# A hybrid streaming-encoder layer on one core: the order of the first loads, two products on zeros, and x scaled on two engines

## The chip, the cores and the metric

The kernel runs on one core of one Trainium2 chip. The metric is the device time of one execution in microseconds; the median of the runs is what counts, and lower is better.

## The reference, cut to what matters

One layer is computed for 512 tokens of width 2048, in float32. The opening, which the change touches, computes the RMS-normalised input `h` and the per-layer embedding `e`:

```
h = rmsnorm(x, g_pre)                 # x: 512 x 2048
proj = h @ w_in                       # feeds a gated DeltaNet branch and a conv branch
... mixers, gates, w_br_a, w_br_b, w_out ...
x = x + rmsnorm(mixed, g_post)
e = p @ w_ple_proj                    # p: 512 x 256, w_ple_proj: 256 x 2048
x = x + rmsnorm(sigmoid(x @ w_ple_gate) * e, g_ple)
```

`e` depends on nothing but `p` and one weight, so the kernel computes it at the very start, while `x` is still arriving, and parks it in DRAM until the end.

## The kernel before, in words

Every large product is a float32 product made from three products of a reduced type: each operand is split into a high part (`hi`, a cast on ACT) and a low part (`lo`, a subtraction on DVE or POOL), and TensorE (PE) multiplies high by high, high by low and low by high into the same bank. Weights stream through `prep()` (lines 115 to 131): a DMA of 512 KB into one of three `raw` tiles, then two pieces, each with a cast into `hi` (L127) and a subtraction into `lo` (L128), into a ring of four `w` tiles. All the DMAs named here are issued from one queue, SP's.

The opening is `load_x()` (lines 226 to 266). Its parts:

- `embed_in()` loads the two halves of the transposed p (`pr`, 256 KB each, L201) and splits them into `ph` (ACT, L203) and `pl` (DVE, L205).
- `embed(j, ...)` for the four column blocks j of `w_ple_proj`: 24 products of 128x512 each (L216, L217, L218), three for each of two depths k and four token tiles, into four banks; then four copies out of the banks, on ACT and DVE in turn (L221). The opening's pool of banks, `xps`, has six.
- For each of the four token tiles of x: two DMAs of 512 KB (L237), two squares with a running sum on ACT (L245), the mean and epsilon on DVE (L247, L248), the power -1/2 on POOL (L250), and two scalings in place on DVE (L252).
- Then 64 transposes on PE (L261), four for each of 16 column tiles, with a scaled copy `hh` on ACT (L264) and its remainder `hl` on DVE (L265). They need the identity matrix (`cst[:, 0:128]`) and the gains in `vec`.
- The 16 blocks of e are written to DRAM by SP (L257), and the rest of the constants is loaded.

After that come `gemm_cm` jobs (products `g`, lines 184 to 188) on w_in, first for the gate of the conv branch, then `z_phase` and everything else. The jobs pull weight pieces from the same ring.

The program order is not the final order. A scheduler goes over the program with a model of its own, starts on each engine whatever comes first in program order among what is ready in that model, and so fixes the order of each engine's queue before the run. The SP queue of before, for instance, holds the second half of p behind the first two DMAs of x, though the program has it ahead of them. On the chip each queue runs in its fixed order.

Of the kernel before, what the change touches and what calls it, by code (L numbers as in the profile page):

```python
# [9 lines left out]
F32 = mybir.dt.float32  # L10
F32R = mybir.dt.float32r
AF = mybir.ActivationFunctionType
ALU = mybir.AluOpType
AX = mybir.AxisListType.X

P = 128
T = 512
NTT = T // P
# [20 lines left out]
V_DW = V_CONV + QKV_TILES * 4  # L39
# [42 lines left out]
def _body(ctx, tc, A, out):  # L82
    nc = tc.nc
    PSUM = bass.MemoryType.PSUM
    mm = nc.tensor.matmul

    const = ctx.enter_context(tc.tile_pool(name="const", bufs=1, side="right"))
    rawp = ctx.enter_context(tc.tile_pool(name="rawp", bufs=3, side="right"))
    ring = ctx.enter_context(tc.tile_pool(name="ring", bufs=4))
    hpool = ctx.enter_context(tc.tile_pool(name="hpool", bufs=32))  # L90
    slots = ctx.enter_context(tc.tile_pool(name="slots", bufs=21, side="right"))
# [2 lines left out]

    cst = const.tile([P, C_COLS], F32, name="cst")
    vec = const.tile([P, V_COLS], F32, name="vec")
    nc.sync.dma_start(cst[:, 0:P], A["consts"][:, 0:P])
    ident = cst[:, C_ID:C_ID + P]
    half_c = const.tile([P, 8], F32, name="half_c")
    nc.gpsimd.memset(half_c, 0.5)  # L100
# [8 lines left out]
    def vv(col, n=1):  # L109
        return vec[:, col:col + n]  # L110


    prep_src = deque()
    prepped = deque()
    low_part = [nc.vector]

    def prep():
        if not prep_src:
            return
        src = prep_src.popleft()  # L120
        raw = rawp.tile([P, 1024], F32, tag="raw", name="raw", bufs=3)
        nc.sync.dma_start(raw, src)
        for q in range(2):
            rq = raw[:, q * T:(q + 1) * T]
            w = ring.tile([P, 1024], F32R, tag="w", name="w")
            hi, lo = w[:, 0:T], w[:, T:]
            nc.scalar.copy(hi, rq)  # L127
            low_part[0].tensor_tensor(lo, rq, hi.bitcast(F32), ALU.subtract)  # L128
            hi_lo[id(hi)] = w.rearrange("p (s c) -> p s c", s=2)
            prepped.append((hi, lo))  # L130
# [64 lines left out]
    pe_dram = dram.tile([4, NTT, P, T], F32, name="pe_dram")  # L195

    def embed_in():
        pT = []
        for k in range(2):
            pr = slots.tile([P, T], F32, tag="s", name="pr")  # L200
            nc.sync.dma_start(pr, A["pT"][k])  # L201
            ph = slots.tile([P, T], F32R, tag="s", name="ph")
            nc.scalar.copy(ph, pr)  # L203
            pl = slots.tile([P, T], F32R, tag="s", name="pl")
            nc.vector.tensor_tensor(pl, pr, ph.bitcast(F32), ALU.subtract)  # L205
            pT.append((ph, pl))
        return pT

    def embed(j, pT, xps):
        ps = [xps.tile([P, T], F32, tag="xp", name="e_ps") for _ in range(NTT)]  # L210
        for k in range(2):
            wh, wl = prepped.popleft()
            lh, ll = pT[k]
            for tt in range(NTT):
                b = slice(tt * P, (tt + 1) * P)
                mm(ps[tt], lh[:, b], wh, start=k == 0, stop=False)  # L216
                mm(ps[tt], lh[:, b], wl, start=False, stop=False)  # L217
                mm(ps[tt], ll[:, b], wh, start=False, stop=k == 1)  # L218
        for tt in range(NTT):
            e = slots.tile([P, T], F32, tag="s", name="e_sb")  # L220
            (nc.vector.tensor_copy if tt % 2 else nc.scalar.copy)(e, ps[tt])  # L221
            e_sb[j, tt] = e
# [3 lines left out]
    def load_x():  # L226
        with tc.tile_pool(name="xin", bufs=1) as xin, tc.tile_pool(name="xps", bufs=6, space=PSUM) as xps:
            xs = []
            H = D // 2
            prep_src.extend(A["w_ple_proj"][j] for j in range(4))  # L230
            prep_src.extend(first_src)
            pT = embed_in()
            prep()
            for tt in range(NTT):
                xt = xin.tile([P, D], F32, name=f"x{tt}")
                for hf in range(2):
                    nc.sync.dma_start(xt[:, hf * H:(hf + 1) * H], A["x"][tt * P:(tt + 1) * P, hf * H:(hf + 1) * H])  # L237
                if tt == 2:
                    nc.sync.dma_start(vec[:, 0:V_DW], A["vecs"][:, 0:V_DW])
                prep()  # L240
                embed(tt, pT, xps)
                ss = small.tile([P, 2], F32, tag="xss", name="xss")
                junk = xin.tile([P, H], F32, name="xjunk")
                for hf in range(2):
                    nc.scalar.activation(junk, xt[:, hf * H:(hf + 1) * H], AF.Square, accum_out=ss[:, hf:hf + 1])  # L245
                ms = small.tile([P, 1], F32, tag="xms", name="xms")
                nc.vector.tensor_tensor(ms, ss[:, 0:1], ss[:, 1:2], ALU.add)  # L247
                nc.vector.tensor_scalar(ms, ms, 1.0 / D, EPS, ALU.mult, ALU.add)  # L248
                rs = small.tile([P, 1], F32, tag="xrs", name="xrs")
                nc.gpsimd.tensor_tensor(rs, ms, mhalf_c[:, 0:1], ALU.pow)  # L250
                for hf in range(2):
                    nc.vector.tensor_scalar(xt[:, hf * H:(hf + 1) * H], xt[:, hf * H:(hf + 1) * H], rs, None, ALU.mult)  # L252
                xs.append(xt)
            nc.sync.dma_start(cst[:, P:], A["consts"][:, P:])
            nc.sync.dma_start(vec[:, V_DW:], A["vecs"][:, V_DW:])
            for (j, tt), e in e_sb.items():
                nc.sync.dma_start(pe_dram[j, tt], e)  # L257
            for k in range(NK):
                ps = xps.tile([P, T], F32, tag="xp", name="xp")
                for tt in range(NTT):  # L260
                    nc.tensor.transpose(ps[:, tt * P:(tt + 1) * P], xs[tt][:, k * P:(k + 1) * P], ident)  # L261
                hh = hpool.tile([P, T], F32R, tag="h", name="hh")
                hl = hpool.tile([P, T], F32R, tag="h", name="hl")
                nc.scalar.activation(hh, ps, AF.Copy, scale=vv(V_GPRE + k))  # L264
                nc.vector.scalar_tensor_tensor(hl, ps, vv(V_GPRE + k), hh.bitcast(F32), ALU.mult, ALU.subtract)  # L265
                hT.append((hh, hl))
# [11 lines left out]

    first_src = [w_in_tile(ZB_TILE0)[0], w_in_tile(ZB_TILE0)[1]]
    load_x()  # L280


# [1055 lines left out]
    def load(jp, pr, q):  # L1338
        n = loads[0]
        loads[0] += 1  # L1340
        if n < 3 or n % 8 in (1, 4, 7):
            raw = rawp.tile([P, 1024], F32, tag="raw", name="raw", bufs=3)
        else:
            raw = s3.tile([P, 1024], F32, tag="rw", name="rw", bufs=5)
        src, blk = WHICH[pr]
        nc.sync.dma_start(raw, src[jp, blk, q])
        sources.append(raw)
# [272 lines left out]
    for tt in range(NTT):  # L1620
# [9 lines left out]
        for j in range(4):  # L1630
            s = e_t4[tt][j]
# [67 lines left out]
```

## Time and profile before

| | us |
|---|---|
| median of three runs | 2446.0 (2445.83 to 2446.65) |
| the profiled execution's own time | 2447.55 |
| its span, first to last instruction | 2445.8 |
| PE busy | 2414.0 (99% of the span) |
| DVE, ACT, POOL busy | 1792.4, 1208.8, 507.0 |
| first product of PE starts | 6.68 |
| embedding products end, transposes start | 32.04 |

The profiled execution took 1.55 us more than the median. Times inside a run are counted from the span's start. In a row of the timeline the first column is the start, the second how long the row lasted; a matmul's length holds the time to drain it, so the pace of PE is read from the distance between starts. "x2" at a row's end says that it stands for two instructions. In brackets stands how long the engine was idle before, and what it waited for.

### The profile page before, as it was taken

The numbers are of one execution on the slowest core, as the hardware profiler recorded it, in microseconds if no ns is written. First come the engines' busy times: TensorE is split into PE (matmuls) and PEld (weight loads), VectorE is DVE, ScalarE is ACT, GpSimd is POOL, SyncE is SP. The second block draws the span as 40 slices with busy tenths as digits, with TensorE's granted clock in tenths as the row PEclk, the third lists the DMA queues.
The fourth block names the chain that finished last, engine by engine and source line by source line (L and its number), as shares of the span: only waits on it lengthen the run. The fifth ranks groups of instructions, "written<-read, shape, count | busy, mean of one in ns | idle before, by whom it ended". The sixth has DMA issues, their size and how long they took to land.

```text
span 2445.8 us, 33732 instructions
## 1 busy us (share of the span) xinstructions
PE 2414.0 (99%) x11962; PEld 1985.5 (81%) x11962; DVE 1792.4 (73%) x3345; ACT 1208.8 (49%) x2357; POOL 507.0 (21%) x531
## 2 busy tenths in 40 slices
PE   8999999999999999999999998999999999999998
PEld 7888888887888888888888887888887888787886
DVE  7877888777677676867777678998998654667644
ACT  6455544554655656455555544454324533554532
POOL 0001110013213021132300005998740000000000
PEclk9999999999999999999999999999999999999999
DMA  7577776666536263556622222443534333665552
GB/s 270 162 199 199 202 201 208 207 162 204 175 119 185 87 185 93 171 168 178 181 90 90 67 91 79 138 137 104 170 118 166 131 122 99 232 216 173 188 173 77
DMA packets 145289, 380.21 MB, mean 155 GB/s; under 512 B 16352, under 2 KB 24800, under 8 KB 145120
## 3 DMA queue, kind: packets, MB, share of 16 engines
q1 hardware_dynamic: 119008, 319.32, 39.4%
q0 software_dynamic: 23808, 54.54, 10.3%
q10 hardware_dynamic: 2304, 4.20, 0.5%
q8 instruction: 94, 1.54, 0.3%
q14 instruction: 75, 0.61, 0.1%
HBM read 329.75 MB, written 48.23 MB: 155 GB/s over the span
## 4 chain that ended last, share of the span: by engine, by line
PE 89%; DVE 3%; POOL 2%; DMA 2%; issue 2%; ACT 2%; SPq 0%; POOLq 0%; DVEq 0%; ACTq 0%
PE g L186 13%; PE g L188 13%; PE g L184 13%; PE zp L423 6%; PE zp L421 6%; PE zp L422 5%; PE yp L1090 4%; PE yp L1094 4%; PE yp L1092 4%; PE f L1382 2%; PE f L1383 2%; PE f L1384 2%; PE f L1548 2%; PE f L1549 2%; PE f L1550 2%
## 5 line engine op out<-in xcount | busy, mean ns | idle before, releaser
L188 PE MATMUL g<-hh,w 128*128 128x512 f32 x1536 | 610.6, 397 | 4.1 <-POOL w L128 4.1
L186 PE MATMUL g<-hl,w 128*128 128x512 f32 x1536 | 611.3, 398 | 0.0
L184 PE MATMUL g<-hh,w 128*128 128x512 f32 x1536 | 609.5, 397 | 0.0
L127 ACT CAST w<-raw 128x512 fp32r<-128x512 f32 x588 | 357.9, 618 | 446.8 <-PE g L188 172.8
L128 DVE TENSOR_TENSOR w<-raw,w 128x512 fp32r<-128x512 f32 x464 | 321.5, 700 | 169.2 <-ACT w L127 166.6
L188 PEld LDWEIGHTS g<-hh,w 128*128 128x128 f32 x1536 | 289.8, 189 | 61.5 <-POOL w L128 5.4
L186 PEld LDWEIGHTS g<-hl,w 128*128 128x128 f32 x1536 | 289.6, 189 | 55.8 <-issue 1.4
L184 PEld LDWEIGHTS g<-hh,w 128*128 128x128 f32 x1536 | 289.9, 189 | 54.7 <-ACT w L127 0.9
L954 DVE SCALAR_TENSOR_TENSOR uc<-up,vec,uc 128x506 f32<-128x506 f32 (+29 forms) x390 | 284.0, 734 | 11.9
L128 POOL TENSOR_TENSOR w<-raw,w 128x512 fp32r<-128x512 f32 x124 | 161.4, 1314 | 136.7 <-DVE uc L954 74.5
L656 DVE SCALAR_TENSOR_TENSOR cv<-g,vec,cv 128x511 f32<-128x511 f32 x144 | 106.4, 739 | 27.2 <-ACT cv L654 26.6
L1090 PE MATMUL yp<-w,uh 128*128 128x512 f32 x256 | 100.2, 392 | 0.7 <-DVE gt L1102 0.7
L1094 PE MATMUL yp<-w,ul 128*128 128x512 f32 x256 | 100.1, 392 | 0.0
L1090 PE MATMUL yp<-w,oh 128*128 128x512 f32 x256 | 100.0, 393 | 0.0
L1092 PE MATMUL yp<-w,uh 128*128 128x512 f32 x256 | 100.0, 391 | 0.0
L1092 PE MATMUL yp<-w,oh 128*128 128x512 f32 x256 | 99.6, 389 | 0.0
L1094 PE MATMUL yp<-w,ol 128*128 128x512 f32 x256 | 99.1, 389 | 0.0
L842 DVE TENSOR_TENSOR prod<-UT,VT 128x2 f32<-128x2 f32 (+30 forms) x248 | 88.4, 356 | 6.5
L1006 POOL DMA_DIRECT2D wsum<-in_w_out x96 | 76.1, 847 | 71.2 <-DMA wsum<-in_w_out 32.9
L1326 POOL TENSOR_TENSOR rmsm<-totm,mhalf_c 128x2 f32<-128x2 f32 x2 | 2.4, 1198 | 378.3 <-DVE totm L1324 378.3
L973 POOL TENSOR_TENSOR uc<-uc,pr 128x511 f32<-128x511 f32 (+29 forms) x60 | 77.8, 1297 | 3.7 <-ACT pr L972 2.5
L1382 PE MATMUL f<-wsp,oph 128*128 128x512 f32 x192 | 75.6, 394 | 1.7 <-ACT wsp L1363 1.7
(386 smaller groups left out, 4952.5 us busy)
## 6 DMA issues: line engine op xcount, KB each, us to landing
raw<-in_w_in SPq DMA_DIRECT2D x194, 512.0 KB, 3.4
wsum<-in_w_out POOLq DMA_DIRECT2D x96, 256.0 KB, 5.4
raw<-in_w_ple_gate SPq DMA_DIRECT2D x40, 512.0 KB, 3.5
wo_sums<-wsum POOLq DMA_DIRECT2D x64, 256.0 KB, 4.1
raw<-in_w_br_a SPq DMA_DIRECT2D x32, 512.0 KB, 3.4
raw<-in_w_br_b SPq DMA_DIRECT2D x32, 512.0 KB, 3.3
raw<-in_w_ga SPq DMA_DIRECT2D x24, 512.0 KB, 4.7
raw<-in_w_gb SPq DMA_DIRECT2D x24, 512.0 KB, 4.5
```

The lines of the kernel that those rows point to most:

```text
L127: nc.scalar.copy(hi, rq)
L128: low_part[0].tensor_tensor(lo, rq, hi.bitcast(F32), ALU.subtract)
L184: mm(ps, wh, rh, start=(k == 0), stop=False)
L186: mm(ps, wh, rl, start=False, stop=False)
L188: mm(ps, wl, rh, start=False, stop=(k == NK - 1))
L421: mm(ps[pr][t], lh, wh, start=q + n == 0, stop=False)
L423: mm(ps[pr][t], lh, wl, start=False, stop=q == 3 and n == 1)
L954: pin(nc.vector.scalar_tensor_tensor(y[:, s:], u[:, 0:T - s], vv(w0 + TAPS - 1 - s), y[:, s:], ALU.mult, ALU.add))
L1090: mm(ps[tt], lh[:, b], wh, start=k == 0, stop=False)
L1092: mm(ps[tt], lh[:, b], wl, start=False, stop=False)
L1094: mm(ps[tt], ll[:, b], wh, start=False, stop=k == NK - 1)
L1382: mm(ps, lh, wh[:, c], start=kk == 0, stop=False)
```

## The change

Six edits, all in the opening:

1. A tile of 128x512 float32 is set to zero on DVE, and PE multiplies it with itself twice at the very start, over 512 and over 384 columns, into a bank that nobody reads.
2. `embed_in()` now also loads the first block of `w_ple_proj`, in two halves: the queue's order in the program is first half of p, first half of the block, second half of p, second half of the block. The casts and subtractions of p and of the block alternate.
3. The DMA of the identity (64 KB), which was the first one, and that of the first part of `vec` (104 KB) stand behind the fourth tile of x.
4. x is loaded by `load(tt)`, ahead of its use; the order in the program is x0, second block, x1, (embed 0), third block, x2, (embed 1), x3, (embed 2), identity, `vec`, fourth block, (embed 3), first piece of w_in. Before, each tile of x was followed by a block, and the last one by w_in.
5. The sum of squares: ACT takes the first half of a tile's columns, DVE the second, with one instruction that multiplies and sums.
6. The scaling: DVE takes the first half, ACT the second.

```diff
-    nc.sync.dma_start(cst[:, 0:P], A["consts"][:, 0:P])
...
     def embed_in():
+        raw = []
+        for k in range(2):
+            raw.append(slots.tile([P, T], F32, tag="s", name="pr"))
+        w0 = rawp.tile([P, 1024], F32, tag="raw", name="raw", bufs=3)
+        nc.sync.dma_start(raw[0], A["pT"][0])
+        for q in range(2):
+            nc.sync.dma_start(w0[:, q * T:(q + 1) * T], A["w_ple_proj"][0][:, q * T:(q + 1) * T])
+            if q == 0:
+                nc.sync.dma_start(raw[1], A["pT"][1])
         pT = []
         for k in range(2):
-            pr = slots.tile([P, T], F32, tag="s", name="pr")
-            nc.sync.dma_start(pr, A["pT"][k])
             ph = slots.tile([P, T], F32R, tag="s", name="ph")
-            nc.scalar.copy(ph, pr)
             pl = slots.tile([P, T], F32R, tag="s", name="pl")
-            nc.vector.tensor_tensor(pl, pr, ph.bitcast(F32), ALU.subtract)
+            nc.scalar.copy(ph, raw[k])
+            w = ring.tile([P, 1024], F32R, tag="w", name="w")
+            hi, lo = w[:, 0:T], w[:, T:]
+            rq = w0[:, k * T:(k + 1) * T]
+            nc.scalar.copy(hi, rq)
+            nc.vector.tensor_tensor(pl, raw[k], ph.bitcast(F32), ALU.subtract)
+            nc.vector.tensor_tensor(lo, rq, hi.bitcast(F32), ALU.subtract)
             pT.append((ph, pl))
+            prepped.append((hi, lo))
...
-            prep_src.extend(A["w_ple_proj"][j] for j in range(4))
+            warm = xin.tile([P, T], F32, name="warm")
+            nc.vector.memset(warm, 0.0)
+            idle = xps.tile([P, T], F32, tag="xp", name="idle")
+            for n in (T, T - P):
+                mm(idle[:, 0:n], warm[:, 0:P], warm[:, 0:n], start=True, stop=True)
+            prep_src.extend(A["w_ple_proj"][j] for j in range(1, 4))
             prep_src.extend(first_src)
-            pT = embed_in()
-            prep()
-            for tt in range(NTT):
+
+            def load(tt):
                 xt = xin.tile([P, D], F32, name=f"x{tt}")
                 for hf in range(2):
                     nc.sync.dma_start(xt[:, hf * H:(hf + 1) * H], A["x"][tt * P:(tt + 1) * P, hf * H:(hf + 1) * H])
-                if tt == 2:
-                    nc.sync.dma_start(vec[:, 0:V_DW], A["vecs"][:, 0:V_DW])
-                prep()
-                embed(tt, pT, xps)
+                xs.append(xt)
+
+            def scale(tt):
+                xt = xs[tt]
                 ss = small.tile([P, 2], F32, tag="xss", name="xss")
                 junk = xin.tile([P, H], F32, name="xjunk")
-                for hf in range(2):
-                    nc.scalar.activation(junk, xt[:, hf * H:(hf + 1) * H], AF.Square, accum_out=ss[:, hf:hf + 1])
+                junk2 = xin.tile([P, H], F32, name="xjunk2")
+                nc.scalar.activation(junk, xt[:, 0:H], AF.Square, accum_out=ss[:, 0:1])
+                nc.vector.scalar_tensor_tensor(junk2, xt[:, H:], 1.0, xt[:, H:], ALU.mult, ALU.mult, accum_out=ss[:, 1:2])
...
-                for hf in range(2):
-                    nc.vector.tensor_scalar(xt[:, hf * H:(hf + 1) * H], xt[:, hf * H:(hf + 1) * H], rs, None, ALU.mult)
-                xs.append(xt)
+                nc.vector.tensor_scalar(xt[:, 0:H], xt[:, 0:H], rs, None, ALU.mult)
+                nc.scalar.activation(xt[:, H:], xt[:, H:], AF.Copy, scale=rs)
+
+            pT = embed_in()
+            load(0)
+            prep()
+            load(1)
+            embed(0, pT, xps)
+            scale(0)
+            prep()
+            load(2)
+            embed(1, pT, xps)
+            scale(1)
+            load(3)
+            embed(2, pT, xps)
+            scale(2)
+            nc.sync.dma_start(cst[:, 0:P], A["consts"][:, 0:P])
+            nc.sync.dma_start(vec[:, 0:V_DW], A["vecs"][:, 0:V_DW])
+            prep()
+            scale(3)
+            embed(3, pT, xps)
+            prep()
             nc.sync.dma_start(cst[:, P:], A["consts"][:, P:])
             nc.sync.dma_start(vec[:, V_DW:], A["vecs"][:, V_DW:])
```

## The prediction, on record before the change was run

> **What bounds the kernel now.** I read first the page's busy times, then the waits of PE, then the opening in the timeline of each engine.
>
> ```profile
> PE 2414.0 (99%) x11962; PEld 1985.5 (81%) x11962; DVE 1792.4 (73%) x3345; ACT 1208.8 (49%) x2357; POOL 507.0 (21%) x531
> PE e_ps L216 <- ACT w L127: 6.7, 1, 6.7
> PE g L188 <- POOL w L128: 4.1, 2, 3.5
> PE po L744 <- DVE O L739: 3.1, 4, 1.0
> ```
>
> PE is the bound: busy 99%, and of its waits 6.7 us are the time before its first product; after the opening the longest are 3.5 us at 1517 and four of at most 1.0 for `po`. So a microsecond won in the opening reaches the end, unless a later engine does not follow. The opening on PE:
>
> ```profile
> 6.68 0.80 PE L216 MATMUL e_ps<-w,ph 128*128 128x512 f32 x1 [6.68 <-ACT w L127]
> 7.41 0.80 PE L217 MATMUL e_ps<-w,ph 128*128 128x512 f32 x1
> ...
> 8.42 0.63 PE L216 MATMUL e_ps<-w,ph 128*128 128x512 f32 x1
> 8.85 0.63 PE L217 MATMUL e_ps<-w,ph 128*128 128x512 f32 x1
> ...
> 11.40 0.40 PE L217 MATMUL e_ps<-w,ph 128*128 128x512 f32 x1
> 11.64 0.40 PE L218 MATMUL e_ps<-w,pl 128*128 128x512 f32 x1
> ...
> 13.36 0.50 PE L218 MATMUL e_ps<-w,pl 128*128 128x512 f32 x1 [0.64 <-DVE pl L205]
> ...
> 32.04 4.79 PE L261 MATMUL xp<-cst,x 128*128 128x128 f32 x40
> ```
>
> Starts lie 0.43 us apart up to 11.40 and 0.23 after. 96 products at 0.229 (the last 72 fill 15.55 to 32.04) would take 22.0 us; they take 25.4. The missing 3.4 are the slow pace from 6.68 to 11.40 (4.72 us for 10 starts, 2.3 at full pace: about 2.3 lost) and the wait for the low part of p's second half, about 1.0 with the slow product behind it. The slow pace is TensorE's clock, as a second place shows, in the timeline and by windows:
>
> ```profile
> 1517.45 0.39 PE L186 MATMUL g<-hl,w 128*128 128x512 f32 x1
> 1521.29 0.79 PE L188 MATMUL g<-hh,w 128*128 128x512 f32 x1 [3.45 <-POOL w L128]
> 1521.88 0.63 PE L184 MATMUL g<-hh,w 128*128 128x512 f32 x1
> ...
> 1526.96 0.40 PE L184 MATMUL g<-hh,w 128*128 128x512 f32 x1
> 1521.00:1523.00 2.00, 1.71 (x4) 1.42 (x5) 1.90 (x4) 0.00 (x0) 2.00 (x3) 0.50 0.78 219
> ```
>
> After 3.45 us of idle PE the same 0.63 rows come at a granted clock of 0.50, for 5.6 us. (For the opening the column of the clock is blank and reads 1.00; there the spacing is the evidence.) So half clock ends 4.7 to 5.6 us after PE begins to work.
>
> **Part by part.** The queue and what waited for it:
>
> ```profile
> 0.74 0.38 SPq L97 DMA_DIRECT2D cst<-in_consts  x1
> 1.17 0.42 SPq L201 DMA_DIRECT2D pr<-in_pT  x1
> 1.64 0.42 SPq L122 DMA_DIRECT2D raw<-in_w_ple_proj  x1
> 2.11 0.91 SPq L237 DMA_DIRECT2D x<-in_x  x2
> 3.06 0.43 SPq L201 DMA_DIRECT2D pr<-in_pT  x1
> 3.53 0.43 SPq L122 DMA_DIRECT2D raw<-in_w_ple_proj  x1
> 3.90 0.62 ACT L203 CAST ph<-pr 128x512 fp32r<-128x512 f32 x1 [1.89 <-DMA pr<-in_pT]
> 6.01 1.14 ACT L127 CAST w<-raw 128x512 fp32r<-128x512 f32 x2 [1.49 <-DMA raw<-in_w_ple_proj]
> 8.36 1.06 ACT L245 ACTIVATE xjunk<-x 128x1024 f32<-128x1024 f32 x1 [1.22 <-DMA x<-in_x]
> 11.54 1.15 ACT L127 CAST w<-raw 128x512 fp32r<-128x512 f32 x2 [0.20 <-DMA raw<-in_w_ple_proj]
> 10.00:20.00 10.00, 9.36 (x38) 7.27 (x38) 7.00 (x15) 7.49 (x15) 1.11 (x2) 1.00 1.01 397
> ```
>
> *Identity away from the front, first block in halves (edits 2, 3).* One issue less ahead shifts the rest by 0.43 us. Before, 320 KB (identity, half of p) had landed at 3.90 and 832 KB at 6.01: 243 KB/us. Now the first half of p and of the block are 512 KB: 3.90 + 192/243 - 0.43 = 4.26. Cast 0.62, semaphore 0.05: first product at 4.95 instead of 6.68. The second waits for the low part as before, 0.73 later, 5.65. Depth k=1 needs 1024 KB: from 832 KB at 6.01 to 1344 KB at 8.36 (first half of x0), 218 KB/us, so 6.46; cast 7.1, low part 7.8. The first 12 products last to 8.2 at full pace or longer, so the wait of 1.0 goes. This part alone: 1.7 + 1.0 = 2.7 us, less what falls due below.
>
> *Zero products (edit 1).* No float32 product of this shape stands in the opening; the nearest is in the later timeline:
>
> ```profile
> 1846.20 1.13 PE L1143 MATMUL sum_ps<-acc,cst 128*128 128x512 f32 x2 [0.63 <-POOL acc L920]
> ...
> 1847.40 0.39 PE L1092 MATMUL yp<-w,oh 128*128 128x512 f32 x1
> ```
>
> From 1846.20 to 1847.40 lie this one and an ordinary product of 0.23: 0.97 us at full clock, at half clock 0.97 x 0.43/0.23 = 1.8; 384 columns 1.35; together about 3.1. The zeroing has no row; the scaling of 128x1024 takes 0.75 on DVE (below), so 512 columns take 0.4 to 0.7, from 0.75 on (ACT's and POOL's first work starts at 0.73). PE works from about 1.3 to 4.4. Cost: nothing, PE has nothing else before 4.95; if they ran to 5.5 they would cost 0.5. Worth: half clock then ends at 1.3 + (4.7 to 5.6) = 6.0 to 6.9, instead of 9.65 to 10.55 counted from 4.95. Block 0's 24 products end at 5.65 + 23 x 0.229 = 10.9, plus 0.46 of each half-clock microsecond after 5.65: 11.1 to 11.5.
>
> The Trainium skill ("TensorE: Matmul & The Clock Gate", Part 1: The HAM clock gate) says the clock opens after a window of about 3.4 us of sustained work, and that the window runs freely, so that the moment differs from run to run. Both places here (4.7 and 5.6) lie between one and two such windows, so the trace agrees. By this rule 3.1 us of zero products fill no window; one that also covers the pause from 4.4 to 4.95 would have to count. If it does, the clock opens at 4.7 to 8.1 and block 0 ends at 10.9 to 12.1, no worse than 0.3 against the sum below; if not, the first rival holds.
>
> *The second block (edit 4).* It stands behind x0 as before. Its 2624th KB had landed at 11.54; now 2560 KB are needed, and the start is 0.43 earlier: 10.95 to 11.4, I take 11.1, since at 397 GB/s the transfers, not the issues, set the pace from 10 on. Cast 11.75, low part 12.4; so PE, free at 11.1 to 11.5, waits, and block 1 runs as if started at 12.2. In before block 1 started at 15.55. Gain 3.35: what is late next is this block.
>
> *The fourth block.* It is moved behind x3, the identity and `vec`. From the second block's end to its own, the queue carries x1, block 2, x2, x3 (3 x 1024 + 512 KB), 64, 104 and 512 KB: 4264 KB at 388 KB/us (397 GB/s), 11.0 us, landing at 22.1; high part 22.75, low part 23.4. Due at 12.2 + 2 x 5.5 = 23.2. So 0.2 to 0.5 is lost; I take 0.25. The third block, 1536 KB after the second, lands at 15.1, due at 17.7: free.
>
> *x on two engines (edits 5, 6).*
>
> ```profile
> L252 DVE TENSOR_SCALAR x<-x,xrs 128x1024 f32<-128x1024 f32 x8 | 5.9, 751 | 2.9 <-POOL xrs L250 2.9
> L265 DVE SCALAR_TENSOR_TENSOR hl<-xp,vec,hh 128x512 fp32r<-128x512 f32 x16 | 10.6, 741 | 0.5 <-ACT hh L264 0.5
> L245 ACT ACTIVATE xjunk<-x 128x1024 f32<-128x1024 f32 x8 | 8.5, 1066 | 1.4 <-DMA x<-in_x 1.4
> ```
>
> Per tile ACT gives up a square (1.07 and 0.19 for reading the sum) and gets a scaled copy, 1.07 by the same row. DVE gives up one scaling (0.75) and gets a multiply with a sum, which has no row: between 0.75 (the scaling) and 1.48 (twice the 512-column row of L265); I take 1.3, nearest in kind. DVE's load per block: two low parts 1.3, two copies 1.3, this 1.3, scaling 0.75, small ones 0.3: 5.0 of the 5.5 us that PE needs per block. It stays covered; at the upper end 5.2. If DVE fell behind, its copies out of the banks would hold PE, six banks against four per block, by some tenths. The last tile of x lands at 20.3 (6144 KB) and takes 1.3 + 0.3 + 0.7 + 1.1, about 24 to 27 with DVE shared, before the transposes at 28.9. Identity and gains land about 20.8, ahead too. Cost on the path: 0 (from 0 to 0.5).
>
> Transposes, `hl` (10.6 us on DVE) and the first `g` products follow the end of the embedding unchanged; the first piece of w_in now lands about 23.4, due 33. Behind that PE waits for nothing longer than 1 us until 1517.
>
> **Sum.** 3.35 - 0.25 = 3.1 us off the profiled execution's 2447.55, so 2444.45; that stands 1.55 above the median, so against 2446.0 the forecast is 2442.9.
>
> **Rivals.**
> *The zero products open no clock* (chance 0.2). For: they stop at about 4.4, half a microsecond before real work. Then half clock lasts to 9.65 to 10.55, block 0 ends at 10.9 + 0.46 x (4.0 to 4.9) = 12.8 to 13.2, block 1 finds its weights; gain 15.55 - 13.0 = 2.55: 2443.45.
> *Nothing is late* (0.12). The second block lands by 10.4 because transfers start sooner. Then 96 products from 4.95: 22.0 + 0.5 for the second product + 0.4 of half clock = 27.85 against 32.04: 4.2, 2441.8. Against: the DMA share is 1.01 from 10 us on.
> *Given back at 1517* (0.06). There PE waits for POOL, and POOL and DVE are busy:
>
> ```profile
> 1500.00:1510.00 10.00, 10.00 (x46) 8.29 (x45) 9.79 (x7) 6.09 (x11) 9.92 (x7) 1.00 0.20 62
> 1487.98 0.33 PE po L744
> ```
>
> If that chain kept its time, all would be lost: 2446.0. Against: the chain of waits starts at PE's own transpose at 1487.98, so it moves with PE.
> *The half clock after 1517 goes* (0.08). It costs 0.46 x 5.6 = 2.6; a shift against the window could shorten it by 2: 2440.9. The same section of the Trainium skill lets a free window do that, here and in the runs before; no row shows it going.
> *The fourth block comes too late* (0.04): slower. The landing at 22.1 would have to slip past 25.4 (wait over 3.1 us) to turn the sign; at a wait of 4 us the clock would close as at 1517: 4 + 2.6 - 3.35 = 3.25 slower, 2449.25. For: it was issued at 10.33 and is now behind 2 MB of x. Against: at 388 KB/us it is 3.3 us early for that.
>
> **How the numbers follow.** The forecast, 0.5, spans 2442.2 to 2443.6. With the first two rivals 0.82 lies between 2441.4 and 2444.3; unknown DVE price, landing and a run-to-run spread of 0.8 widen this to 2440.8 to 2445.2. A change of 0.2% (4.9 us) is about what can be told from none: below 2441.1 lie most of the fourth rival and little else, 0.08; above 2450.9 almost nothing, 0.03; within, 0.89.
>
> **What would show it.** First embedding product at 4.6 to 5.4; the spacing falls to 0.23 by 7 (rival one: after 9); PE waits on the high part of the second block near 11.1, no wait for `pl`; transposes start at 28.5 to 29.5; `cst` and `vec` issue behind x. What would make it wrong most likely: the scheduler's order on a queue differing from the program's (second block ahead of x0, or a copy out of a bank held behind x on DVE), or other orders far behind the opening.

## The result, and the profile after

The changed kernel takes 2450.47 us (median of 19 runs, 2448.99 to 2452.91) against 2445.93 (19 runs, 2443.88 to 2448.16): ratio 1.002, 95% interval 1.0013 to 1.0027. It is 4.5 us slower; forecast were 2442.9 and a range of 2440.8 to 2445.2, with a chance of 0.03 for anything above 2450.9; the measured time lies just below that and far outside the range. One run of before in the second set of experiments took 2976.07 us, in a slow state of the chip, and the ratios leave it out. The profiled execution of after took 2451.02 by its own time (span 2449.2), that of before 2447.55.

PE's opening in the timeline of after (start, duration, engine, line, operation; in brackets idle time before and its releaser), and one stretch by windows (length, then busy time of PE, PEld, DVE, ACT and POOL, granted clock, DMA share):

```profile
1.45 3.35 PE L246 MATMUL idle<-warm 128*128 128x512 f32 x4 [1.45 <-DVE warm L243]
5.00 2.07 PE L228 MATMUL e_ps<-w,ph 128*128 128x512 f32 x4 [0.20 <-ACT w L214]
6.88 0.63 PE L229 MATMUL e_ps<-w,ph 128*128 128x512 f32 x1
7.30 0.55 PE L230 MATMUL e_ps<-w,pl 128*128 128x512 f32 x1
7.69 0.39 PE L229 MATMUL e_ps<-w,ph 128*128 128x512 f32 x1
...
11.88 0.97 PE L228 MATMUL e_ps<-w,ph 128*128 128x512 f32 x3
...
23.34 0.40 PE L230 MATMUL e_ps<-w,pl 128*128 128x512 f32 x1
28.04 2.04 PE L228 MATMUL e_ps<-w,ph 128*128 128x512 f32 x4 [4.30 <-ACT w L126]
29.88 0.63 PE L229 MATMUL e_ps<-w,ph 128*128 128x512 f32 x1
...
35.24 0.93 PE L297 MATMUL xp<-cst,x 128*128 128x128 f32 x7
```
```profile
28.00:32.00 4.00, 3.96 (x10) 3.16 (x11) 2.50 (x4) 1.55 (x3) 0.00 (x0) 0.57 1.01 387
```

Up to 23.34 this is nearly the forecast: first product at 5.00, full pace from 7.7 (forecast by 7), second block at 11.88, no wait for the low part of p. There PE stands 2.97 us ahead of before (whose third block ends 25 products ahead of its transposes at 32.04: 26.31). Then it waits 4.30 us for the high part of the fourth block and works at half clock afterwards (a mean of 0.57 from 28 to 32). The next product starts 4.70 after the last instead of 0.23, 4.47 lost; block 4's 24 products take 7.20 instead of 5.5, 1.70 lost. Transposes: 35.24 instead of 32.04. From 85 us on that distance stays between 2.8 and 3.9 to the end, some products around 1490 apart.

What PE waited for is seen on the other queues: the issue of the fourth block on SP, then ACT's timeline, DVE's and POOL's; behind them the time from that issue to the landing, from the view of its tile.

```profile
13.81 0.33 SPq L121 DMA_DIRECT2D raw<-in_w_ple_proj  x1
...
22.25 1.15 ACT L269 ACTIVATE x<-x,xrs 128x1024 f32<-128x1024 f32 x1
23.31 0.57 ACT L233 COPY e_sb<-e_ps 128x512 f32<-128x512 f32 x1
26.33 1.15 ACT L269 ACTIVATE x<-x,xrs 128x1024 f32<-128x1024 f32 x1 [2.46 <-POOL xrs L267]
27.39 2.16 ACT L126 CAST w<-raw 128x512 fp32r<-128x512 f32 x4
...
22.25 0.76 DVE L268 TENSOR_SCALAR x<-x,xrs 128x1024 f32<-128x1024 f32 x1 [0.73 <-POOL xrs L267]
22.92 0.69 DVE L233 COPY e_sb<-e_ps 128x512 f32<-128x512 f32 x1
23.52 1.22 DVE L262 SCALAR_TENSOR_TENSOR xjunk<-x 128x1024 f32<-128x1024 f32 x1
...
26.34 0.75 DVE L268 TENSOR_SCALAR x<-x,xrs 128x1024 f32<-128x1024 f32 x1 [0.73 <-POOL xrs L267]
28.02 2.50 DVE L127 TENSOR_TENSOR w<-raw,w 128x512 fp32r<-128x512 f32 x4 [0.93 <-ACT w L126]
...
25.75 0.55 POOL L267 TENSOR_TENSOR xrs<-xms,mhalf_c 128x1 f32<-128x1 f32 x1 [3.53 <-DVE xms L265]
```
```profile
DMA to landing us min/median/max: 8.1/8.1/8.1
```

The weights landed at 13.81 + 8.1 = 21.9. From 23.9 to 26.33 ACT did nothing: its next instruction was the scaling of the last x tile, which needs that tile's factor from POOL, POOL needs the sums from DVE, and DVE began its square only at 23.52, behind the scaling of the tile before. The casts stand behind that scaling, though the program text has the fourth block's preparation ahead of it. The fixed order on ACT, not the transfer, made PE wait.

A second profile of the changed kernel (own time 2454.02):

> The changed kernel, profiled again. By the cause found (casts of block 4 behind x3's scaling on ACT): a wait of PE for the high part of the fourth block of 3.5 to 5 us again, transposes at 34.5 to 36 (35.24 in the first profile), and half clock behind it for 3.4 or 6.8 us. If the wait were an accident of the one run, it would be below 2 and the transposes before 32.

```profile
29.20 2.08 PE L228 MATMUL e_ps<-w,ph 128*128 128x512 f32 x4 [4.30 <-ACT w L126]
31.07 0.63 PE L229 MATMUL e_ps<-w,ph 128*128 128x512 f32 x1
```
```profile
28.00:32.00 4.00, 2.80 (x7) 2.25 (x8) 2.74 (x5) 2.71 (x5) 0.00 (x0) 0.50 0.96 366
32.00:35.00 3.00, 3.00 (x9) 2.38 (x8) 0.00 (x0) 0.00 (x0) 0.00 (x0) 0.56 0.00 0
```

The same wait, to the hundredth. The half clock behind it now lasts 6.8 us (3.4 in the first, by the trace's record of the granted clock), and the transposes start at 37.31, later than the 34.5 to 36 expected. So the wait belongs to the order, the half clock's length to the run.

### The profile page after: what moved, and what is told of

Its sections match the earlier page's. It is cut to its first block, busy times and chain, and to the rows that moved or that the text cites. A ratio compares the mean times of both kernels' runs of the same rounds, so it can differ in the third digit from the quotient of the medians.

```text
span 2449.2 us, 33738 instructions
## 1 busy us (share of the span) xinstructions
PE 2418.3 (99%) x11966; PEld 1987.7 (81%) x11966; DVE 1794.5 (73%) x3350; ACT 1209.7 (49%) x2353; POOL 508.5 (21%) x531
## 4 chain that ended last, share of the span: by engine, by line
PE 90%; DVE 3%; issue 2%; POOL 2%; ACT 1%; DMA 1%; SPq 0%; POOLq 0%; DVEq 0%; ACTq 0%
PE g L185 13%; PE g L187 13%; PE g L183 13%; PE zp L459 6%; PE zp L458 6%; PE zp L457 6%; PE yp L1126 4%; PE yp L1130 4%; PE yp L1128 4%; PE f L1418 2%; PE f L1419 2%; PE f L1420 2%; PE f L1586 2%; PE f L1584 2%; PE f L1585 2%
```

## The experiments

Medians are of 11 runs (19 for the changed kernel), with before measured on the same chip (33 runs in each set; 2445.86 in the first, 2446.14 in the second, 2445.91 in the third). Times on PE are starts in the one profile of each kernel; where there are several, all stand.

| kernel | median us | ratio, 95% interval | first embedding product | transposes | first `zp` |
|---|---|---|---|---|---|
| before (three profiles) | 2445.9 | | 6.68, 6.09, 6.04 | 32.04, 30.84, 31.02 | 93.90, 92.72, 92.88 |
| changed (two profiles) | 2450.47 | 1.0013 to 1.0027 | 5.00, 5.33 | 35.24, 37.31 | 96.99, 99.06 |
| block4_ahead | 2449.16 | 1.0006 to 1.0024 | 5.12 | 29.56 | 96.67 |
| x3_on_dve | 2450.08 | 1.0009 to 1.0027 | 5.01 | 34.45 (two at 25.25) | 96.15 |
| fill_the_wait | 2448.76 | 1.0003 to 1.0020 | 4.73 | 33.77 | 95.52 |
| split_undone | 2448.34 | 0.9999 to 1.0017 | 5.01 | 30.44 | 94.22 |
| both_ahead (two profiles) | 2445.85 | 0.9992 to 1.0009 | 5.02, 5.01 | 28.97, 28.53 | 92.33, 91.89 |
| split_undone_both | 2446.17 | 0.9995 to 1.0013 | 5.54 | 31.28 | 93.46 |
| split_undone_both_no_zeros | 2445.92 | 0.9992 to 1.0010 | 4.91 | 29.71 | 91.74 |
| before_second_piece | 2446.48 | 0.9995 to 1.0013 | 6.07 | 32.06 | 94.07 |
| both_ahead_pool_lows | 2445.62 | 0.9990 to 1.0008 | 5.07 | 28.34 | 91.35 |
| split_undone_both_pool_lows | 2445.75 | 0.9993 to 1.0010 | 4.97 | 30.02 | 92.23 |
| before_pool_lows | 2446.64 | 0.9992 to 1.0010 | 6.74 | 32.56 | 94.46 |
| split_alone | 2445.92 | 0.9993 to 1.0010 | 6.01 | 30.24 | 92.11 |

**block4_ahead**: the changed kernel with the fourth block loaded and prepared ahead of the last x tile.

```
 scale(1)
+prep()
 load(3)
 ...
-prep()
 scale(3)
```

> The changed kernel with one edit: the fourth embedding block's load and preparation stand ahead of the fourth tile of x in the program (they stood behind it, the identity and vec). Theory A (PE waited 4.3 us for the fourth block because ACT's queue had its cast behind the scaled copy of the last x tile, and the clock fell in that wait): no wait ahead of the fourth block, transposes start at 28.8 to 29.5 instead of 35.24, no half clock behind the first, about 2442.9 (2442 to 2444), 3 us faster than before. Theory C (the loss lies behind the opening, in changed orders or in half clock near 1490): the opening ends 6 us earlier, but the time stays above 2447.

The wait at 28 is gone and the transposes start at 29.56, 5.68 ahead of the changed kernel; the time falls by 1.3 only, so theory A's transposes nearly came (28.8 to 29.5) and its time did not; theory C's time held, for a place that it did not name. What was won is lost at a second place, where PE of the changed kernel, being later, does not wait; it is seen in the timelines of PE and DVE:

```profile
46.54 0.80 PE L187 MATMUL g<-hh,w 128*128 128x512 f32 x1 [2.48 <-DVE w L127]
47.13 0.63 PE L183 MATMUL g<-hh,w 128*128 128x512 f32 x1
...
42.73 2.48 DVE L344 TENSOR_TENSOR hf<-hh,hl 128x512 f32<-128x512 f32 x4
45.13 0.75 DVE L344 TENSOR_TENSOR zsf<-hf 128x256 f32<-128x256 f32 x2
45.80 1.28 DVE L127 TENSOR_TENSOR w<-raw,w 128x512 fp32r<-128x512 f32 x2
```

The low parts of w_in's second piece stand behind four additions and two subtractions of the z stage. In before they stand behind one addition, and DVE has no gap there:

```profile
33.40 10.63 DVE L265 SCALAR_TENSOR_TENSOR hl<-xp,vec,hh 128x512 fp32r<-128x512 f32 x16 [0.47 <-ACT hh L264]
43.94 0.68 DVE L308 TENSOR_TENSOR hf<-hh,hl 128x512 f32<-128x512 f32 x1
44.54 1.29 DVE L128 TENSOR_TENSOR w<-raw,w 128x512 fp32r<-128x512 f32 x2
```

PE idles 2.48 us and works at half clock again (0.63 rows, 3.4 us).

**x3_on_dve**: the changed kernel, but both halves of the last x tile scaled on DVE, so that nothing on ACT waits for its factor.

```
-nc.scalar.activation(xt[:, H:], xt[:, H:], AF.Copy, scale=rs)
+if tt == 3: nc.vector.tensor_scalar(xt[:, H:], xt[:, H:], rs, None, ALU.mult)
+else: nc.scalar.activation(xt[:, H:], xt[:, H:], AF.Copy, scale=rs)
```

> The changed kernel with one edit: the second half of the last x tile is scaled on DVE, so ACT has nothing to wait for ahead of the fourth block's cast; the order of the DMAs is as in the changed kernel. Theory A: the cast follows the copies out of block 3 at about 23.9, PE waits about 1 us instead of 4.3 and stays at full clock, transposes at 30 to 30.5, time 2444 to 2446, some 5 us less than the changed kernel. Theory B (the weights themselves land late, being behind x, identity and vec): nothing moves, the wait stays at 4 us and the time at 2450.

```profile
23.53 2.18 ACT L126 CAST w<-raw 128x512 fp32r<-128x512 f32 x4
...
26.76 0.75 DVE L270 TENSOR_SCALAR x<-x,xrs 128x1024 f32<-128x1024 f32 x1
27.42 1.89 DVE L127 TENSOR_TENSOR w<-raw,w 128x512 fp32r<-128x512 f32 x3
...
28.16 0.50 PE L229 MATMUL e_ps<-w,ph 128*128 128x512 f32 x1 [2.53 <-DVE w L127]
```

Neither expectation held. The casts moved up to 23.53, but the low parts stand behind the same tile's square and scalings on DVE, and PE waited there (0.70 for ACT and 2.53 for DVE). It rules out the landing, for ACT cast at 23.5, and shows that both queues held the weights behind x3. The time, 2450.08, is hardly less than the changed kernel's.

**fill_the_wait**: the changed kernel with four float32 products of a landed x tile on PE between the third and the fourth block (eight records in the trace); nothing reads them.

```
+fill = gps.tile([P, T], F32, tag="g", name="fill")
+for _ in range(4):
+    mm(fill, xs[2][:, 0:P], xs[2][:, 0:T], start=True, stop=True)
 embed(3, pT, xps)
```

> The changed kernel with four float32 products of 512 columns more, on a tile of x, into a bank that nobody reads, standing between block 3 and block 4 in PE's queue; 0.85 us each, 3.4 us in all, they lie inside the wait of 4.3 us. ACT's order is as in the changed kernel. Theory A: the wait for the cast stays where it is (fourth block at about 28.0), but the clock does not fall, so the fourth block's 24 products take 5.5 instead of 7.2 us and the transposes start at 33.6 to 33.9; time 2448.5 to 2449.2, some 1.6 us less than the changed kernel. If the half clock there is no matter of idle PE, the time stays at 2450.5.

```profile
23.64 3.59 PE L289 MATMUL fill<-x 128*128 128x512 f32 x8
28.11 0.98 PE L228 MATMUL e_ps<-w,ph 128*128 128x512 f32 x3 [0.88 <-ACT w L126]
28.93 0.41 PE L229 MATMUL e_ps<-w,ph 128*128 128x512 f32 x1
```

Block 4 starts no earlier (28.11), but at full clock: transposes 1.47 sooner, time 1.7 less, as theory A has it. So the half clock behind the wait is its own part of the loss, about 1.5 us.

**split_undone**: the kernel before with the zero products and edits 2 and 3 (the identity behind the third tile of x); x squared on ACT and scaled on DVE, and the loop with its order of loads, as before. Two things of the changed kernel are undone at once here, the split and the late fourth block. Against the changed kernel, cut to the split:

```
-nc.vector.scalar_tensor_tensor(junk2, ...)   (squares of both halves on ACT)
-nc.scalar.activation(xt[:, H:], ...)         (scalings of both halves on DVE)
```

> Before, with the zero products, p and the first block first and the identity behind x's third tile; x is squared on ACT and scaled on DVE alone as before, and each block's preparation follows a tile of x as before. Theory A: ACT has no scaled copy of x that could stand ahead of a cast, so no wait for the fourth block; transposes at 28.5 to 29.5, time 2442 to 2444, as with the fourth block ahead. If the split itself is worth something, this one is slower than that by as much; I expect no difference beyond 0.5.

The fourth block is in time and the transposes start at 30.44; PE's waits in the opening, 0.65 and 0.75 us, are now for the second block. The second place remains: PE waits 2.00 us up to 45.59 for the low part of w_in's second piece. Theory A's time did not come; the interval, 0.9999 to 1.0017, does not tell this kernel from before. Its profile has a further 2.6 us of delay between 566 and 758 us that no other profile shows.

**Both places at once**: both_ahead is block4_ahead, split_undone_both is split_undone, each with the second piece of w_in prepared ahead of the last constants and the writes of e; then the latter without the zero products, and before with the second piece alone.

```
+prep()
 nc.sync.dma_start(cst[:, P:], A["consts"][:, P:])
```

> The changed kernel with the fourth block ahead of x3 and, besides, the second piece of w_in loaded ahead of the constants and of the writes of e (it stood behind them). Theory D (the opening is won, but is given back wherever the model that fixes the queues expects a transfer later than it lands and puts other work of DVE or ACT ahead of a weight's preparation; with the fourth block ahead, that place was the first g products, where four additions and two subtractions of the z stage stood ahead of the low parts on DVE): both pieces are prepared ahead of hl, PE waits nowhere up to 85, transposes at 29 to 29.6, the lead of 2.5 us over before is still there at 85, time 2442.5 to 2444 against 2445.9. Rival E (the gain is lost behind 85 us, in half clock near 1490 and 1520): the lead at 85 is there, and the time still 2446 or more.

> As split_undone (before, with the zero products, p and first block first, identity later), with the second piece of w_in ahead of the e writes. Theory D: no wait of 2.0 us near 45, lead of 1.5 to 2.5 us at 85, time 2443.5 to 2445. Rival E: 2446 or more, with the lead at 85.

> As the one before it, without the two products on zeros. The clock then opens 3.4 to 6.8 us behind the first product at 5.0, between 8.4 and 11.8, instead of 5 to 7.7; the transposes start some 1 us later (30.5 to 31.5), and the time is 0.5 to 1.5 us more than with the zeros. If the zeros open nothing, no difference.

> Before, with one edit: the second piece of w_in is loaded ahead of the constants and the writes of e. It is to show whether this edit has a worth of its own: PE had no wait there, so theory D expects transposes at 32 and the time of before, 2445.9 within 0.7. If it is faster by more than 1, the gain of the two kernels above is not the opening's.

both_ahead is 4.6 us faster than the changed kernel: 2445.85. So with the two orders mended all of the loss is gone. But theory D's time, 2442.5 to 2444, did not come: it is no faster than before (2446.14; the interval allows a gain of 2.0 us), though its transposes start where the prediction put them, at 28.97 and 28.53. Where that went stands in its timelines:

```profile
28.97 2.83 PE L298 MATMUL xp<-cst,x 128*128 128x128 f32 x24
32.45 0.49 PE L183 MATMUL g<-hh,w 128*128 128x512 f32 x1 [0.65 <-ACT hh L301]
33.60 0.66 PE L298 MATMUL xp<-cst,x 128*128 128x128 f32 x4 [0.67 <-DVE hl L302]
...
31.00 1.89 DVE L127 TENSOR_TENSOR w<-raw,w 128x512 fp32r<-128x512 f32 x3
32.80 10.62 DVE L302 SCALAR_TENSOR_TENSOR hl<-xp,vec,hh 128x512 fp32r<-128x512 f32 x16
43.34 2.49 DVE L345 TENSOR_TENSOR hf<-hh,hl 128x512 f32<-128x512 f32 x4
```

DVE is still at the low parts of the weights when the transposes come; `hl` runs from 32.80 to 43.34, before's from 33.40 to 43.94. PE is three microseconds early and waits for an engine that is 0.6 early. split_undone_both fits neither theory: no wait near 45, but a lead of 0.4 only at `zp`, and 2446.17. The zero products show no worth: 2446.17 with, 2445.92 without; by their intervals a worth of 1 us could hide in that, and in the one profile with them the clock opened late, at 10.5. before_second_piece, the control, is no faster than before, as expected.

**Low parts on POOL**: in both_ahead, split_undone_both and before_second_piece the low parts of w_in's first two pieces are put on POOL, idle there; **split_alone** is before with edits 5 and 6 only.

```
+low_part[0] = nc.gpsimd
 prep()
 prep()
+low_part[0] = nc.vector
```

> Edit: as both_ahead (the change, with block 4 and w_in's second piece issued, cast and split in time), and the low parts of the pieces prepared by the last two calls (block 4 and w_in's first and second piece as far as these calls reach) are computed on POOL instead of DVE. Theory A (behind the embedding DVE is the co-bound: in both_ahead it works on low parts of 0.64 each from 31.0 to 32.8 before the first hl, and the 16 hl products of 0.74 end at 43.34 against 44.03 before, though the transposes start 3.07 earlier): freed of about four low parts DVE starts hl about 1.8 earlier, hl end near 41.5, the g products follow, and the lead at about 85 us is 2.5 to 3.1 instead of 1.57. Time: both_ahead's 2445.85 less 0.9 to 1.5, so 2444.3 to 2445.0. Theory B (the lead is lost again further on whatever happens here, as both_ahead's lead of 1.9 at 551 us did not show in the median): the lead at 85 us grows as in A, the time stays 2445.5 to 2446.3. Theory C (POOL is too slow for them: about 1.3 each): PE waits for POOL's low parts, the lead at 85 us is below 1.5 and the time 2446 to 2448.

> Edit: as split_undone_both (zero products and edits 2 and 3; x squared on ACT and scaled on DVE as in the kernel before; w_in's second piece ahead), with the same low parts on POOL. Theory A: the lead at 85 us grows from 0.44 to 1.5 to 2.5; time 2445.0 to 2445.6 against split_undone_both's 2446.17. Theory B: the lead grows, the time stays 2445.8 to 2446.5. Theory C: no larger lead, 2446 to 2448.

> Edit: the kernel before, w_in's second piece ahead and the same low parts on POOL; the opening on PE as before. The control for the two others: PE is not released earlier, DVE is freed of the same low parts. Theory A (PE and DVE bound this stretch in turns: in before no wait of PE there is longer than 0.2): no gain worth naming, 2446.0 to 2446.7, lead at 85 us 0 to 0.7. Theory D (DVE alone bounds the stretch, the opening on PE is worth nothing): the lead at 85 us is 1.5 or more and the time equals that of both_ahead_pool_lows within 0.5.

> Edit: the kernel before with edits 5 and 6 alone (the second half of each x tile squared on DVE, scaled on ACT; loop, loads and embedding as before). My prediction's step: cost 0 to 0.5. Theory A (the split costs only where it stands ahead of a block's weight preparation; here the fourth block is issued ahead of x3, so its casts are ahead as well): transposes within 0.5 of before's 32.04, time 2446 to 2447. Theory E (the split itself overloads DVE in the opening: its squares are 1.22 us where one scaling of 0.75 is given up, and all else follows later): PE waits for DVE's low parts or copies in the opening, transposes 1 or more late, and 2447 to 2449.

```profile
31.80 10.63 DVE L304 SCALAR_TENSOR_TENSOR hl<-xp,vec,hh 128x512 fp32r<-128x512 f32 x16 [2.56 <-ACT hh L303]
```

In both_ahead_pool_lows DVE sits idle for 2.56 us, waiting for ACT, which was casting the weights; `hl` starts 1.0 earlier, not 1.8, and `zp` at 91.35 is the earliest of all. The time, 2445.62, is no different; theory B's time held, without showing why. split_undone_both_pool_lows has theory A's lead (1.67), and its time, 2445.75, lies between A's and B's. In before_pool_lows, the control, PE is 0.5 late against before's first profile (POOL's work slows the last scalings of x, see the end) and the time unchanged, against theory D. split_alone shows the split of x harmless where the fourth block is issued ahead of x3: no wait above 0.2 in the opening behind the first product, transposes at 30.24, time 2445.92.

**More profiles of the same kernels.** Six kernels that PE's starts put 0.4 to 2.6 us ahead at `zp` have medians within 0.4 us of before. Was the one profile of before late?

> The kernel before, profiled again. Theory 1 (the profiled opening of before was late by chance): first product nearer to 6.0 than 6.68, transposes at 30 to 31 instead of 32.04, first zp product at 92 to 93 instead of 93.90. Theory 2 (the opening is repeatable, leads are lost behind 92 us): 93.4 to 94.4 as in before, before_second_piece (94.07) and before_pool_lows (94.46).

> The kernel before, profiled a third time; as for the second profile: theory 1 first zp at 92 to 93, theory 2 at 93.4 to 94.4. The time from there to the last f product was 2342.1 in the first profile; by theory 1 it is 2341 to 2344 here as in the other kernels, by theory 2 below 2341.5.

> both_ahead, profiled again. Both theories: transposes at 28.5 to 30, first zp product at 91.5 to 93 (92.33 in the first). Theory 2: from there to the last f product 2342.5 or more (2341.4 in the first), so that the lead is lost; theory 1: 2340.5 to 2342.5.

Rows of the second, then the third profile of before:

```profile
6.09 0.79 PE L216 MATMUL e_ps<-w,ph 128*128 128x512 f32 x1 [6.09 <-ACT w L127]
30.84 2.34 PE L261 MATMUL xp<-cst,x 128*128 128x128 f32 x20
32.20 10.63 DVE L265 SCALAR_TENSOR_TENSOR hl<-xp,vec,hh 128x512 fp32r<-128x512 f32 x16 [0.47 <-ACT hh L264]
```
```profile
6.04 0.79 PE L216 MATMUL e_ps<-w,ph 128*128 128x512 f32 x1 [6.04 <-ACT w L127]
31.02 2.24 PE L261 MATMUL xp<-cst,x 128*128 128x128 f32 x19
```

Theory 1 holds for two of three: transposes at 30.84 and 31.02, `zp` at 92.72 and 92.88. Against these both_ahead's `zp` (92.33, 91.89) is 0.7 early on average, and before's `hl` (from 32.20 and 32.38) starts no later than both_ahead's (32.80 and 32.37), but for a hundredth. That is below what these runs can tell. But before's opening also came late in two other profiles that keep its first loads (94.07, 94.46), so one opening differs from the next by over 1 us. Theory 2 did not come out: from `zp` to the last `f` product both_ahead took 2341.4 and 2341.9, not more than before (2342.1, 2343.0 and 2342.3) but less. So in these single executions the lead is kept to the end; the first profiles' own times are 2445.20 against 2447.55, those of the repeated ones, all on one other chip, 2445.25 against 2447.20 and 2446.73. The medians, 2445.85 and 2446.14, do not show it. Whether both_ahead is faster by something up to 2 us stays open.

## Why the prediction was wrong

*The first block (edits 2, 3)*: right. First product at 5.00 against 4.95; the wait for the low part of p is gone. *The zero products*: placed as said (1.45 to 4.8, no cost). The clock opened at 7.63, not at 6.0 to 6.9, and in the second profile at 10.7, where the first rival's case held; over the runs they are worth nothing that can be measured. The two profiles differ in the pause behind the zeros, 0.20 and 0.52 us, and by the figures of the last section such a pause can decide it. *The second block*: right, 11.88 against 12.2; its cast began at 11.20, with the landing forecast for 11.1.

*The fourth block* is the step that failed. "Landing at 22.1" measured 21.9. "High part 22.75, low part 23.4" took for granted that ACT and DVE are free at the landing; the cast began at 27.39. The term of -0.25 measured -6.2 (4.47 of waiting and 1.70 of half clock; 7.1 in the second profile). Its root lies in two steps that were never laid side by side. The sum has the cast of the fourth block at 22.1; the next step, *x on two engines*, has the last tile's scaling between 24 and 27 (it ended at 27.5), half of it now on ACT, the engine of that cast. Which of the two stands first on ACT's queue, and on DVE's, was not asked. "Cost on the path: 0 (from 0 to 0.5)" was worked out from loads, 5.0 of 5.5 us per block on DVE. The load was right (4.6 to 4.7 in the second and third block), and split_alone bears out that the split by itself, with before's order of loads, costs nothing. Nor is ACT's share of the split the whole cause: in x3_on_dve ACT has no scaling of the last tile, and DVE's square and scalings of it hold the low parts back instead. What freed both queues, with the split kept, was the fourth block ahead of the last tile (block4_ahead). No run has the late fourth block with the split wholly undone. The prediction named the order on a queue as the likeliest source of an error; it put no price on it.

*The rival "the fourth block comes too late"* had the mechanism on PE, a wait of about 4 us and then half clock, and a time of 2449.25; its condition, a landing past 25.4, did not occur. A chance of 0.04 for transfers alone was too little for everything that lies between a landing and PE.

*"Behind that PE waits for nothing longer than 1 us until 1517"* was read off the kernel before. It held in the changed kernel, whose PE came late, and did not survive an earlier PE. In block4_ahead and split_undone PE waits 2.5 and 2.0 us for w_in's second piece; with that mended, DVE's chain of `hl` takes most of the lead by `zp`. Before was just in time there; its DVE was busy without a gap, which the waits of PE can't show.

*The sum* started from one profiled execution whose transposes were 1.0 to 1.2 us later than in two others. Of the 3.1 us predicted, both_ahead has 2.0 to 2.4 at the transposes against those two (30.93 less 28.97 and 28.53), and 0.7 is left at `zp`; against the mean of all three it is 2.6 and 1.1. The loss adds up: `zp` in the changed kernel starts at 98.0 (mean of two) against 93.2 (of three), 4.9 late; the median is 4.5 late. *Given back at 1517* had no part in it: the wait for POOL there, 3.4 to 3.7 us, stands in every profile. *The half clock after 1517* did not go either: the record has 6.8 us of it before and, in two parts of 3.4 near 1492 and 1527, after. *Nothing is late* did not occur: the second block landed at 11.2, not by 10.4.

## What to carry to other kernels

A landing time is not a ready time: for each moved transfer, list what stands ahead of its first consumer on that engine's queue, and what that instruction itself waits for. Before a stage is fed sooner, look whether another engine is busy without a gap just behind it; PE's list of waits is silent about an engine that is only just in time. Where a wait of some 2.5 us, or several shorter ones within a few microseconds, can arise on PE, price the half clock behind it too, and take the baseline of an opening from several profiles.

## What the runs showed of the hardware

A wait of 2.5 us (block4_ahead, x3_on_dve) was enough for half clock afterwards, as was one of 4.3; after the wait of 2.00 us in split_undone the clock stayed full. The prediction had only 3.45 us as evidence. The half clock lasted 3.4 or 6.8 us in the trace's record of the granted clock, for the same 4.30 us of waiting. The Trainium skill ("TensorE: Matmul & The Clock Gate", Part 1: The HAM clock gate) gives a free-running window of about 3.4 us; one or two windows agree with these two lengths.

That record says more. In each of the eighteen profiles all its changes lie whole multiples of 3.41 us apart; in the changed kernel's first the opening ones are 7.63, 28.11 and 31.53. Cut PE's timeline into these steps and add up its idle time in each. At half clock, the clock opened at the end of all 46 steps with up to 0.45 us of idle time and of none of the 47 with 0.52 or more. At full clock, it fell at the end of 28 steps, with 1.80 to 3.35 us of idle time, and no other step had more than 1.93, so the border lies at 1.8 to 1.9. These limits were worked out afterwards, from matmul ends that are modelled, and no run was made to test them, but they fit what was told above. The two waits of 4.30 us fell differently into the steps (each row below is one step, of the first and of the second profile): in the first the wait was over when the half clock began, and one busy step ended it; in the second the wait reached 1.39 us into the step at half clock, and it took another. The wait of 2.00 us in split_undone had a border inside, at 44.63, and put about 1 us into each step. At 1492.43 the clock fell in the changed kernel's first profile after two waits of 0.99 and 0.87 us.

```profile
28.11:31.53 3.42, 3.42 (x8) 2.72 (x9) 2.41 (x4) 1.44 (x3) 0.00 (x0) 0.50 1.05 404
27.81:31.22 3.41, 2.02 (x5) 1.65 (x6) 2.47 (x5) 2.90 (x5) 0.00 (x0) 0.50 1.06 407
```

By the record and the spacing of the products the clock of the opening opened at 4.4 to 7.6 us in nine of eleven profiles with zero products, at 10.5 and 10.7 in two, and at 9.6 to 11.4 in the seven without. In the nine, PE paused for at most 0.39 us between the zeros and the first embedding product; in the two, for 0.73 and 0.52. So the zeros do bring the clock forward when hardly any pause follows them; by these limits the prediction's own pause, 4.4 to 4.95, could have been too long. What they bring is given back as told.

DVE's scaling of x, 0.75 us otherwise, took more than twice that while POOL computed low parts. In before_pool_lows:

```profile
23.98 1.42 DVE L253 TENSOR_SCALAR x<-x,xrs 128x1024 f32<-128x1024 f32 x2 [0.73 <-POOL xrs L251]
29.48 3.47 DVE L253 TENSOR_SCALAR x<-x,xrs 128x1024 f32<-128x1024 f32 x2 [0.73 <-POOL xrs L251]
29.40 5.94 POOL L128 TENSOR_TENSOR w<-raw,w 128x512 fp32r<-128x512 f32 x4
```

The same two scalings take 1.42 and 3.47 us. The Trainium skill ("SBUF — State Buffer", SBUF: two separate sides) tells of a port pair that DVE's faster modes and GpSimd hold in turn, the other standing still. The trace agrees so far that each slows the other: POOL's four subtractions take 5.94 us here and 5.00 in both_ahead_pool_lows.
